# A row-wise log-sum-exp: the first piece's sum by way of PSUM, and two rows summed by halves instead of by a reduce

## The chip, the cores and the metric

The kernel runs on one core of a Trainium2 chip. The metric is device time in microseconds (us), from the start of the program to its end on that core; lower is better. Before the change it is 162.02 us, the median of three runs.

## What is computed

The input `x` is 32 x 512 x 1024 in float32, that is 16384 rows of 1024 elements. For each row:

```
max_x = np.max(x, axis=-1, keepdims=True)
out   = max_x.squeeze(-1) + np.log(np.sum(np.exp(x - max_x), axis=-1))
```

The kernel takes the exps without the maximum first and checks the sums. If every sum is between 1e-15 and 1e15, `log(sum(exp(x)))` is the answer; otherwise a second path, under an `If`, does the whole with the maximum. The data here never take that path.

## The kernel before

**Tiling.** Each of the 128 partitions has 128 rows (`NC`), numbered 0 to 127 in the order of loading; W = 112 divides them. Rows below 112 lie together in memory for each partition, and so do the last 16, so that the results go out in two stores. The on-chip buffer `ring` has room for 48 rows per partition. `LOADS` lists 18 loads with their size in rows and what is done with them. All are issued by SyncE (SP) on one DMA queue, the first six large (16 to 12.5 rows), the later ones ever smaller, down to about half a row. A load waits until the rows that it overwrites have been summed.

**What is done with a row.** ScalarE (ACT) takes the exp in place (L212), one instruction for each group of rows. Then the group is summed in one of these ways, each with a letter in `LOADS`:
- `R`: VectorE (DVE) reduces the rows whole, in one instruction (L223).
- `F`: GpSimd (POOL) adds the second half of each row to its first half (L217), "folds" it, and VectorE reduces the halves later (L159, in `reduce_folded`). The fold is put on a list; VectorE reduces what is on the list at the end of the next `R` or `T` group, or ahead of the next fold.
- `T`: VectorE takes the rows one by one: one instruction adds the two halves of a row and sums the result (L232), a 128x512 `SCALAR_TENSOR_TENSOR` with an accumulator. The accumulator is then read out to `sumexp` by an instruction of its own (`DVE_READ_ACCUMULATOR`).
- `Y` and `Z`: the last row, number 127, comes in two loads of 544 and 480 elements. ScalarE takes their exps into PSUM (`last_exp`) and sums them by its own accumulator (L190), which is read out by an `ACTIVATION_READ_ACCUMULATOR`: the first piece's sum to `sumexp[:, 127]`, the second's to `sumexp[:, 128]`.

**Order.** The code issues in the order of the loads, and each engine works through its own queue in that order; semaphores that count each engine's finished instructions tie them together. `Counted.wait` (L39 to L44) leaves a wait out if the engine has waited for the same count or a later one before. The ninth load, `(5.5, "F4 R2")`, holds rows 106 to 111, the last below W: four are folded, two reduced. From row 112 on, all groups but the last row are `T`: 4, 3, 3, 2, 1, 1 and 1 rows.

**The end.** When the groups up to row 118 are issued, ScalarE takes the Ln of rows 0 to 111 (L251), SyncE stores them (L259), and VectorE checks the sums of rows 0 to 118 (L134, L139). TensorE counts: each later row's sum is added up over the partitions in the PSUM tile `count` (`add_up`, L148), and so is the number of sums that were out of bounds (`bad`, L144 and L280). After the last row, ScalarE takes the Ln of rows 112 to 126 (L262) and of row 127 (L264, with the first piece's sum as bias), and SyncE stores the 16 columns (L268). VectorE checks rows 119 to 127 (L274), TensorE adds what is left, and VectorE compares the count with its bound (`fine`, L283). ScalarE and VectorE load that truth value, branch, and tell SyncE, which waits for the stores and ends the program.

Of the kernel before, what the change touches and what calls it, by code (L numbers as in the profile page):

```python
# [16 lines left out]

LOADS = [
# [3 lines left out]
]  # L22

# [24 lines left out]
def kernel(  # L48
# [5 lines left out]
    nc = tc.nc  # L54
# [4 lines left out]
    P = nc.NUM_PARTITIONS  # L59
    fp32 = mybir.dt.float32  # L60
# [8 lines left out]
    NC = n // P  # L69
    H = d // 2  # L70
    W = NC - B
    LAST = NC - 1
# [6 lines left out]
    def source(e0, size):  # L79
        assert e0 >= W * d or e0 + size <= W * d  # L80
        return x_rest[:, e0 - W * d : e0 - W * d + size] if e0 >= W * d else x_rows[:, e0 : e0 + size]
# [8 lines left out]
    def sbuf(name, cols, dtype=fp32, rows=P):  # L90
        return nc.alloc_sbuf_tensor(name, [rows, cols], dtype).ap()

    ring = sbuf("ring", RING * d)
    sumexp = sbuf("sumexp", NC + 1)
# [4 lines left out]
    ones = sbuf("ones", 1)  # L99
    fine = sbuf("fine", 1, i32, 1)  # L100
    last_exp = nc.alloc_psum_tensor("last_exp", [P, d], fp32).ap()
    count = nc.alloc_psum_tensor("count", [1, 1], fp32).ap()

    landed = [nc.alloc_semaphore(f"landed{i}") for i in range(len(loads))]
    act = Counted(nc, nc.scalar, "act")
    dve = Counted(nc, nc.vector, "dve")
# [15 lines left out]
    def load(i, here, done_before, size):  # L122
        for a, b, who, at in users:
            if a < here + size and b > here:
                sp.wait(who, at)
        users[:] = [u for u in users if not (u[0] < here + size and u[1] > here)]
        return nc.sync.dma_start(  # L127
            out=ring[:, here : here + size], in_=source(done_before, size)
        ).then_inc(landed[i], 16)

    def check_early():
        dve.wait(act, summed_by_act)
        dve.wait(dve, dve.n)
        dve.did(nc.vector.tensor_scalar(  # L134
            out=clamped[:, 0:LATE], in0=sumexp[:, 0:LATE],
            scalar1=LOW, scalar2=HIGH, op0=ALU.max, op1=ALU.min,
        ))
        dve.wait(dve, dve.n)
        dve.did(nc.vector.scalar_tensor_tensor(  # L139
            out=clamped[:, 0:LATE], in0=clamped[:, 0:LATE], scalar=0.0, in1=sumexp[:, 0:LATE],  # L140
            op0=ALU.bypass, op1=ALU.not_equal, accum_out=bad[:, 0:1],
        ))
        pe.wait(dve, dve.n)
        pe.did(nc.tensor.matmul(count, lhsT=bad[:, 0:1], rhs=far, start=True, stop=False))  # L144

    def add_up(c, who, **kw):
        pe.wait(*who)
        return pe.did(nc.tensor.matmul(count, lhsT=ones, rhs=sumexp[:, c : c + 1], **kw))  # L148
# [3 lines left out]
    def reduce_folded():  # L152

        nonlocal early_sum
        while folded:
            c0, s0, p0, n0 = folded.pop(0)
            halves = ring[:, p0 : p0 + s0 * d].rearrange("p (c d) -> p c d", d=d)[:, :, 0:H]
            dve.wait(pool, n0)
            at = dve.did(nc.vector.reduce_sum(  # L159
                out=sumexp[:, c0 : c0 + s0], in_=halves, axis=AX.X  # L160
            ))
            users.append((p0, p0 + s0 * d, dve, at))
            if c0 < W:
                early_sum = at

    c = 0
# [7 lines left out]
    for i, (size, ops) in enumerate(loads):  # L174
        if here + size > RING * d:
            assert here == p
            p = here = 0
        if any(q < here + size and q + t * d > here for _, t, q, _ in folded):
            reduce_folded()
        dma = load(i, here, done_before, size)  # L180
        first_load = first_load or dma.ins
        end = here + size
        done_before += size
        act.wait(landed[i], 16)
        for k, (how, s) in enumerate(ops):
            rows = ring[:, p : p + s * d].rearrange("p (c d) -> p c d", d=d)
            if how in "YZ":

                assert c == LAST and (how == "Z" or here == p)
                at = act.did(nc.scalar.activation(  # L190
                    out=last_exp[:, here - p : end - p], in_=ring[:, here:end], func=AF.Exp,
                    accum_out=sumexp[:, LAST : NC] if how == "Y" else sumexp[:, NC : NC + 1],
                ))
                here = end
                if how == "Y":
                    first_piece = at
                summed_by_act = at
            elif how == "A":
                assert here == p
                v = ring[:, p : p + d]  # L200
                at = act.did(nc.scalar.activation(
                    out=v, in_=v, func=AF.Exp, accum_out=sumexp[:, c : c + 1]
                ))
                here += d
                users.append((p, p + d, act, at))
                summed_by_act = at
                who = (act, at)
            else:

                upto = end if k + 1 == len(ops) and c + s < LAST else p + s * d  # L210
                v = ring[:, here:upto]
                at = act.did(nc.scalar.activation(out=v, in_=v, func=AF.Exp))  # L212
                here = upto
            if how == "F":
                reduce_folded()
                pool.wait(act, at)
                at = pool.did(nc.gpsimd.tensor_tensor(  # L217
                    out=rows[:, :, 0:H], in0=rows[:, :, 0:H], in1=rows[:, :, H:d], op=ALU.add
                ))
                folded.append((c, s, p, at))  # L220
            elif how == "R":
                dve.wait(act, at)
                who = (dve, dve.did(nc.vector.reduce_sum(  # L223
                    out=sumexp[:, c : c + s], in_=rows, axis=AX.X
                )))
                users.append((p, p + s * d, *who))
            elif how == "T":
                reduce_folded()
                dve.wait(act, at)
                for r in range(s):  # L230
                    lo = rows[:, r, 0:H]
                    who = (dve, dve.did(nc.vector.scalar_tensor_tensor(  # L232
                        out=lo, in0=lo, scalar=1.0, in1=rows[:, r, H:d],
                        op0=ALU.mult, op1=ALU.add, accum_out=sumexp[:, c + r : c + r + 1],
                    )))
                    users.append((p + r * d, p + (r + 1) * d, *who))
                    if c + r >= LATE:
                        add_up(c + r, who, start=False, stop=False)
            if how == "A" and c >= LATE:
                add_up(c, who, start=False, stop=False)  # L240
            if how in "RT":
                if c < W:
                    early_sum = dve.n
                reduce_folded()
            c += s
            p += s * d
            if c == LATE:

                act.wait(dve, early_sum)
                act.wait(act, early_act)  # L250
                ln_early = act.did(nc.scalar.activation(  # L251
                    out=res[:, 0:W], in_=sumexp[:, 0:W], func=AF.Ln
                ))
                check_early()
            if c <= W:
                early_act = summed_by_act
        assert here == end
# [7 lines left out]
        out=res[:, LAST:NC], in_=sumexp[:, NC : NC + 1], func=AF.Ln, bias=sumexp[:, LAST:NC]  # L265
# [3 lines left out]

    dve.wait(act, first_piece)
    dve.wait(dve, dve.n)
    dve.did(nc.vector.scalar_tensor_tensor(  # L274
        out=clamped[:, LATE:NC], in0=sumexp[:, LATE:NC], scalar=LOW,
        in1=sumexp[:, LATE:NC], op0=ALU.max, op1=ALU.not_equal, accum_out=bad[:, 1:2],
    ))
    add_up(LAST, (act, first_piece), start=False, stop=False)
    pe.wait(dve, dve.n)
    pe.did(nc.tensor.matmul(count, lhsT=bad[:, 1:2], rhs=far, start=False, stop=False))  # L280
    at = add_up(NC, (act, summed_by_act), start=False, stop=True)
    dve.wait(pe, at)
    at = dve.did(nc.vector.tensor_scalar(out=fine, in0=count, scalar1=HIGH, scalar2=None, op0=ALU.is_lt))  # L283
# [6 lines left out]
    with nc.If(all_fine < 1):  # L290
# [5 lines left out]
        for c0 in range(0, NC, RING):  # L296
# [6 lines left out]
            for c1, c2 in ((c0, edge), (edge, c0 + s)):  # L303
                if c1 == c2:
                    continue
                nc.scalar.dma_start(
                    out=ring[:, (c1 - c0) * d : (c2 - c0) * d],
                    in_=source(c1 * d, (c2 - c1) * d),
# [4 lines left out]
                out=neg, in_=v, op=ALU.max, axis=AX.X, negate=True  # L313
# [3 lines left out]
                out=v, in0=v, in1=neg[:, :, None].to_broadcast([P, s, d])  # L317
# [5 lines left out]
                out=sumexp[:, c0 : c0 + s], in_=v, axis=AX.X  # L323
# [71 lines left out]
```

## Time and profile before

| | us |
|---|---|
| median of three runs | 162.02 (161.79, 162.02, 163.18) |
| the profiled execution | 161.82 |
| its span, first to last instruction | 160.5 |
| VectorE busy in the span | 113.8 |
| ScalarE busy | 114.5 |
| GpSimd busy | 37.2 |
| mean DMA rate over the span | 419 GB/s |

An engine's busy time is the time in which it worked on an instruction. Where an instruction begins before the one ahead of it has left the pipeline, the two overlap in the list, so that a row's length is more than the distance to the next row's start. The timeline lists instructions in order of their start, with their length, their engine, the line of the code, and the output and input tiles; in brackets stands how long the engine was idle before and for whom it waited.

### The profile page before, as it was taken

The numbers are of one execution on the slowest core, as the hardware profiler recorded it, in microseconds if no ns is written. First come the engines' busy times: TensorE is split into PE (matmuls) and PEld (weight loads), VectorE is DVE, ScalarE is ACT, GpSimd is POOL, SyncE is SP. The second block draws the span as 40 slices with busy tenths as digits, with TensorE's granted clock in tenths as the row PEclk, the third lists the DMA queues.
The fourth block names the chain that finished last, engine by engine and source line by source line (L and its number), as shares of the span: only waits on it lengthen the run. The fifth ranks groups of instructions, "written<-read, shape, count | busy, mean of one in ns | idle before, by whom it ended". The sixth has DMA issues, their size and how long they took to land.

```text
span 160.5 us, 208 instructions
## 1 busy us (share of the span) xinstructions
PE 2.1 (1%) x24; PEld 1.0 (1%) x24; DVE 113.8 (71%) x53; ACT 114.5 (71%) x30; POOL 37.2 (23%) x10
## 2 busy tenths in 40 slices
PE   0000000000000000000000000000000000000022
PEld 0000000000000000000000000000000000000011
DVE  0000000009999499994999859959999999999995
ACT  3000059990799708995099949992999979989996
POOL 0000000000000000000000993690004969873000
DMA  8996996996996996996999999999999999999992
GB/s 278 506 523 278 506 523 261 523 523 261 523 523 261 523 506 278 523 490 294 482 441 441 441 425 408 408 408 498 423 423 404 406 426 421 449 406 427 417 407 80
DMA packets 2880, 67.18 MB, mean 419 GB/s; under 512 B 576, under 2 KB 704, under 8 KB 1344
## 3 DMA queue, kind: packets, MB, share of 16 engines
q1 hardware_dynamic: 2880, 67.18, 97.7%
HBM read 67.11 MB, written 0.07 MB: 419 GB/s over the span
## 4 chain that ended last, share of the span: by engine, by line
DMA 55%; DVE 22%; ACT 20%; SPq 0%; issue 0%; PE 0%; DVEq 0%
DMA ring<-in_x_dram 55%; ACT ring L212 20%; DVE sumexp L223 15%; DVE ring L232 4%; DVE sumexp L159 2%; SPq L127 0%; DVE clamped L139 0%; DVE clamped L134 0%; PE count L148 0%; PE count L280 0%; DVE clamped L274 0%; DVE fine L283 0%; DVEq L44 0%
## 5 line engine op out<-in xcount | busy, mean ns | idle before, releaser
L212 ACT ACTIVATE ring<-ring 128x16384 f32<-128x16384 f32 (+16 forms) x22 | 111.6, 5121 | 43.1 <-DMA ring<-in_x_dram 43.1
L223 DVE TENSOR_REDUCE sumexp<-ring 128x16 f32<-128x16384 f32 (+4 forms) x9 | 85.6, 9514 | 43.1 <-ACT ring L212 43.1
L217 POOL TENSOR_TENSOR ring<-ring 128x2048 f32<-128x2048 f32 (+2 forms) x6 | 37.0, 6171 | 108.5 <-ACT ring L212 108.5
L159 DVE TENSOR_REDUCE sumexp<-ring 128x4 f32<-128x2048 f32 (+2 forms) x6 | 18.4, 3078 | 0.1
L232 DVE SCALAR_TENSOR_TENSOR ring<-ring 128x512 f32<-128x512 f32 x15 | 9.5, 687 | 0.0
L115 ACT ACT_TABLE_LOAD x1 | 1.3, 1283 | 1.4 <-PEq L57 1.4
L144 PE MATMUL count<-far,bad 128*1 128x1 f32 x2 | 0.2, 164 | 153.3 <-DVE clamped L139 153.3
L148 PE MATMUL count<-sumexp,ones 128*1 128x1 f32 x20 | 1.8, 164 | 3.5 <-DVE ring L232 3.4
L232 DVE DVE_READ_ACCUMULATOR ring<-ring 128x1 f32 x15 | 1.2, 83 | 0.0
L190 ACT ACTIVATE last_exp<-ring 128x544 f32<-128x544 f32 (+1 forms) x2 | 1.2, 578 | 0.0
L116 DVE MEMSET ones<- 128x1 f32 x1 | 0.1, 59 | 1.5 <-PEq L57 1.5
L144 PEld LDWEIGHTS count<-far,bad 128*1 128x1 f32 x2 | 0.1, 82 | 153.3 <-DVE clamped L139 153.3
L148 PEld LDWEIGHTS count<-sumexp,ones 128*1 128x1 f32 x20 | 0.8, 81 | 4.4 <-DVE ring L232 4.3
L283 DVE TENSOR_SCALAR fine<-count 1x1 int32<-1x1 f32 x1 | 0.1, 145 | 0.5 <-PE count L148 0.5
L190 ACT ACTIVATION_READ_ACCUMULATOR last_exp<-ring 128x1 f32 x2 | 0.4, 186 | 0.0
L139 DVE SCALAR_TENSOR_TENSOR clamped<-clamped,sumexp 128x119 f32<-128x119 f32 x1 | 0.3, 283 | 0.0
L264 ACT ACTIVATE res<-sumexp 128x1 f32<-128x1 f32 x1 | 0.3, 294 | 0.0
L251 ACT ACTIVATE res<-sumexp 128x112 f32<-128x112 f32 x1 | 0.3, 280 | 0.0
L134 DVE TENSOR_SCALAR clamped<-sumexp 128x119 f32<-128x119 f32 x1 | 0.2, 223 | 0.0
L274 DVE SCALAR_TENSOR_TENSOR clamped<-sumexp 128x9 f32<-128x9 f32 x1 | 0.2, 169 | 0.1
L262 ACT ACTIVATE res<-sumexp 128x15 f32<-128x15 f32 x1 | 0.2, 198 | 0.0
L280 PE MATMUL count<-far,bad 128*1 128x1 f32 x2 | 0.2, 164 | 0.0
(8 smaller groups left out, 0.7 us busy)
## 6 DMA issues: line engine op xcount, KB each, us to landing
ring<-in_x_dram SPq DMA_DIRECT2D x1, 6912.0 KB, 23.9
ring<-in_x_dram SPq DMA_DIRECT2D x1, 6400.0 KB, 19.7
ring<-in_x_dram SPq DMA_DIRECT2D x1, 4608.0 KB, 15.9
ring<-in_x_dram SPq DMA_DIRECT2D x1, 3840.0 KB, 12.4
ring<-in_x_dram SPq DMA_DIRECT2D x1, 2816.0 KB, 18.7
ring<-in_x_dram SPq DMA_DIRECT2D x1, 2352.0 KB, 23.8
ring<-in_x_dram SPq DMA_DIRECT2D x1, 1664.0 KB, 21.1
ring<-in_x_dram SPq DMA_DIRECT2D x1, 1280.0 KB, 23.7
```

The costliest lines, as they stand in the source:

```text
L115: nc.scalar.preload_act_table_set("natural_log_exp_and_others")
L139: dve.did(nc.vector.scalar_tensor_tensor(out=clamped[:, 0:LATE], in0=clamped[:, 0:LATE], scalar=0.0, in1=sumexp[:, 0:LATE], op0=ALU.bypass ...
L144: pe.did(nc.tensor.matmul(count, lhsT=bad[:, 0:1], rhs=far, start=True, stop=False))
L148: return pe.did(nc.tensor.matmul(count, lhsT=ones, rhs=sumexp[:, c : c + 1], **kw))
L159: at = dve.did(nc.vector.reduce_sum(out=sumexp[:, c0 : c0 + s0], in_=halves, axis=AX.X))
L190: at = act.did(nc.scalar.activation(out=last_exp[:, here - p : end - p], in_=ring[:, here:end], func=AF.Exp, accum_out=sumexp[:, LAST : NC ...
L212: at = act.did(nc.scalar.activation(out=v, in_=v, func=AF.Exp))
L217: at = pool.did(nc.gpsimd.tensor_tensor(out=rows[:, :, 0:H], in0=rows[:, :, 0:H], in1=rows[:, :, H:d], op=ALU.add))
L223: who = (dve, dve.did(nc.vector.reduce_sum(out=sumexp[:, c : c + s], in_=rows, axis=AX.X)))
L232: who = (dve, dve.did(nc.vector.scalar_tensor_tensor(out=lo, in0=lo, scalar=1.0, in1=rows[:, r, H:d], op0=ALU.mult, op1=ALU.add, accum_out ...
L251: ln_early = act.did(nc.scalar.activation(out=res[:, 0:W], in_=sumexp[:, 0:W], func=AF.Ln))
L264: ln_last = act.did(nc.scalar.activation(out=res[:, LAST:NC], in_=sumexp[:, NC : NC + 1], func=AF.Ln, bias=sumexp[:, LAST:NC]))
```

## The change

The ninth load's two rows ahead of row 112 become a `T` group: two instructions that add halves and sum, instead of one reduce. The four folded rows of the same load are still reduced after them: for a `T` group ahead of row 112 the list of folds isn't emptied first. The sum of the last row's first piece (`Y`) is read out to a new PSUM tile, `first_sum`, instead of to `sumexp[:, 127]`. VectorE copies it from there to `sumexp[:, 127]`, behind the last `T` row on its queue, once ScalarE has it. VectorE's wait for ScalarE ahead of L274 goes, since the copy has waited, and TensorE, which adds that column up, waits for the copy instead of for ScalarE.

```diff
@@ -17,7 +17,7 @@
 
 LOADS = [
     (16, "R16"), (16, "R16"), (16, "R16"), (16, "F9 R7"), (13.5, "F6 R7"), (12.5, "R7 F6"),
-    (9, "R5 F4"), (7.5, "F4 R3"), (5.5, "F4 R2"), (4.59375, "T4"), (3.25, "T3"), (2.5, "T3"),
+    (9, "R5 F4"), (7.5, "F4 R3"), (5.5, "F4 T2"), (4.59375, "T4"), (3.25, "T3"), (2.5, "T3"),
     (1.78125, "T2"), (1.25, "T1"), (0.9375, "T1"), (0.6875, "T1"), (0.53125, "Y"), (0.46875, "Z"),
 ]
 
@@ -99,6 +99,7 @@
     ones = sbuf("ones", 1)
     fine = sbuf("fine", 1, i32, 1)
     last_exp = nc.alloc_psum_tensor("last_exp", [P, d], fp32).ap()
+    first_sum = nc.alloc_psum_tensor("first_sum", [P, 1], fp32).ap()
     count = nc.alloc_psum_tensor("count", [1, 1], fp32).ap()
 
     landed = [nc.alloc_semaphore(f"landed{i}") for i in range(len(loads))]
@@ -189,11 +190,12 @@
                 assert c == LAST and (how == "Z" or here == p)
                 at = act.did(nc.scalar.activation(
                     out=last_exp[:, here - p : end - p], in_=ring[:, here:end], func=AF.Exp,
-                    accum_out=sumexp[:, LAST : NC] if how == "Y" else sumexp[:, NC : NC + 1],
+                    accum_out=first_sum if how == "Y" else sumexp[:, NC : NC + 1],
                 ))
                 here = end
                 if how == "Y":
-                    first_piece = at
+                    dve.wait(act, at)
+                    first_piece = dve.did(nc.vector.tensor_copy(out=sumexp[:, LAST:NC], in_=first_sum))
                 summed_by_act = at
             elif how == "A":
                 assert here == p
@@ -225,7 +227,8 @@
                 )))
                 users.append((p, p + s * d, *who))
             elif how == "T":
-                reduce_folded()
+                if c >= W:
+                    reduce_folded()
                 dve.wait(act, at)
                 for r in range(s):
                     lo = rows[:, r, 0:H]
@@ -269,13 +272,12 @@
 
 
 
-    dve.wait(act, first_piece)
     dve.wait(dve, dve.n)
     dve.did(nc.vector.scalar_tensor_tensor(
         out=clamped[:, LATE:NC], in0=sumexp[:, LATE:NC], scalar=LOW,
         in1=sumexp[:, LATE:NC], op0=ALU.max, op1=ALU.not_equal, accum_out=bad[:, 1:2],
     ))
-    add_up(LAST, (act, first_piece), start=False, stop=False)
+    add_up(LAST, (dve, first_piece), start=False, stop=False)
     pe.wait(dve, dve.n)
     pe.did(nc.tensor.matmul(count, lhsT=bad[:, 1:2], rhs=far, start=False, stop=False))
     at = add_up(NC, (act, summed_by_act), start=False, stop=True)
```

## The prediction

> **What bounds the kernel now.** I read the chain of waits first, to learn which engine sets the end and from when. The chain in order of time (start, length, what), last half:
>
> ```profile
> 115.75 3.27 DVE sumexp L159
> ...
> 119.88 23.82 DMA ring<-in_x_dram
> 143.70 0.02 issue
> 143.72 7.00 ACT ring L212 x2
> 150.72 0.02 issue
> 150.75 1.94 DVE ring L232 x6
> ...
> 153.26 4.96 DVE ring L232 x16
> ...
> 158.32 0.19 DVE clamped L274 x2
> ...
> 158.98 0.14 DVE fine L283
> ```
>
> Up to 143.70 the loads set the pace. From there the exps (L212) run back to back, and the rows that VectorE (DVE) sums by halves (L232) follow close behind them, so the end has two chains that finish together. One is the check: the last row sum, L274, two pairs of matmuls, `fine` at 158.98. The other is the store, and it needs the timeline of the last stretch (start, length, engine, line):
>
> ```profile
> 157.51 0.69 DVE L232 SCALAR_TENSOR_TENSOR ring<-ring 128x512 f32<-128x512 f32 x1
> ...
> 157.93 0.19 ACT L190 ACTIVATION_READ_ACCUMULATOR last_exp<-ring 128x1 f32 x1
> 158.02 0.55 ACT L190 ACTIVATE last_exp<-ring 128x480 f32<-128x480 f32 x1
> 158.12 0.08 DVE L232 DVE_READ_ACCUMULATOR ring<-ring 128x1 f32 x1
> ...
> 158.60 0.20 ACT L262 ACTIVATE res<-sumexp 128x15 f32<-128x15 f32 x1
> 158.73 0.29 ACT L264 ACTIVATE res<-sumexp 128x1 f32<-128x1 f32 x1
> ...
> 159.05 0.34 SPq L268 DMA_DIRECT2D out_dram<-res  x1
> ```
>
> The list of DMA issues gives this last store 1.4 us to landing: 159.05 + 1.4 = 160.45, the span's 160.5. The check's chain has 160.5 - 159.12 = 1.4 us left after `fine` for the load of the truth value, the branch and SyncE's closing waits. Nothing shows more than a few hundredths of slack on either, so I take both as limiting. On the store's chain VectorE has room: its last row sum is out at 158.12 + 0.08 = 158.20 and ScalarE (ACT) asks for it at 158.60, 0.40 later.
>
> Then the place of the second edit, the timeline before the first L232:
>
> ```profile
> 141.40 4.54 POOL L217 TENSOR_TENSOR ring<-ring 128x2048 f32<-128x2048 f32 x1 [1.72 <-ACT ring L212]
> 141.44 2.28 DVE L159 TENSOR_REDUCE sumexp<-ring 128x4 f32<-128x2048 f32 x1
> 143.63 2.28 DVE L223 TENSOR_REDUCE sumexp<-ring 128x2 f32<-128x2048 f32 x1
> 143.72 6.99 ACT L212 ACTIVATE ring<-ring 128x4704 f32<-128x4704 f32 x2 [0.60 <-DMA ring<-in_x_dram]
> 145.97 2.29 DVE L159 TENSOR_REDUCE sumexp<-ring 128x4 f32<-128x2048 f32 x1
> 148.18 0.68 DVE L232 SCALAR_TENSOR_TENSOR ring<-ring 128x512 f32<-128x512 f32 x1
> 148.78 0.08 DVE L232 DVE_READ_ACCUMULATOR ring<-ring 128x1 f32 x1
> ```
>
> GpSimd (POOL) folds four rows of the 5.5-row load from 141.40 to 141.40 + 4.54 = 145.94. VectorE reduces the other two at 143.63 (the piece that changes), and at 145.97, 0.03 after POOL, reduces the folded four. The rows by halves begin at 148.18. POOL is done for good by then: in the whole trace no L232 lies beside an L217.
>
> **The two rows by halves.** Removed: one reduce, 143.63 to 145.91, 2.28 us. Added: two L232 with their accumulator reads; rows follow one another by 149.40 - 148.78 = 0.62, over several rows 0.612, so 1.22 us. No DMA is added, and all loads are issued by then, so no ring space is freed for anything. VectorE is 2.28 - 1.22 = 1.06 less busy, but that can't be a gain: the next instruction on its queue is the reduce of the folded rows, and that waits for POOL until 145.94 anyway. The cover of the saved 1.06 is POOL's fold; the most that can come forward is 0.03.
>
> The unknown is what POOL's fold and the two rows do to each other, since they now lie side by side. Lower bound: nothing. The nearest row is L223 beside L217: POOL's three folds of this size take 4.53 to 4.55 whatever VectorE reduces meanwhile, and the reduce of 2048 elements takes 2.28 both with POOL running (141.44) and without (145.97). Upper bound: the two exclude each other, and the rows' 1.22 us is added to POOL's 145.94. It does not matter which gives way: if the rows wait they run from 145.94 to 147.16, and if POOL waits its fold ends at 147.16. Below nothing there is only the 0.03.
>
> I take the upper bound, for a reason that lies in the rows. A reduce draws 2048 elements in 2.28 us, 1.11 ns each. L232 draws two halves, 1024 elements, in 0.612 us, 0.60 ns each. So L232 reads by a second path that the reduce leaves idle, and the undisturbed reduces say nothing of that path. POOL's fold draws 4096 elements in 4.54 us, 1.11 ns each, the rate of one path all the time. If the second path of VectorE is the one that POOL uses, there is little room in it for both.
>
> [...]
>
> With the upper bound the reduce of the folded rows starts at 147.16 + 0.03 = 147.19 instead of 145.97, 1.22 late. Who waits behind it: the Ln of the first 112 rows (L251) needs it, but ScalarE only comes to it at 150.62, and the reduce ended at 148.26, so 2.36 us of cover hide the delay. All L232 rows are queued behind it. They start at 149.40 and run without a pause until the end, since the exps are then ahead. Two small waits for ScalarE swallow part: the fifth row could start at 150.62 (rows start with the accumulator read of the one before) and did at 150.75, 0.13; the last could at 157.46 and did at 157.51, 0.05. So 1.22 - 0.18 = 1.04 arrives at the last row sum: 158.20 becomes 159.24.
>
> **The first piece's sum by way of PSUM.** The accumulator read of L190 now writes PSUM; the row lasts 0.19 either way as far as the trace can say, and the next exp starts 0.09 after its start, so I cost it at nothing. Added: a copy of 128x1 on VectorE, behind the last row and ahead of L274. The trace has no such copy. Bounds: 0.06 (L116's 128x1 memset, 59 ns) and 0.145 (L283, which reads PSUM); I take 0.145, since this one reads PSUM too. The last row's accumulator read starts at 158.12 + 1.04 = 159.16, the copy with it, and ends at 159.31; a wait on VectorE's own result costs 0.04 (152.67 to L134 at 152.71), so L274 starts at 159.35. Before, L274 paid for two waits, 158.20 to 158.32; now the wait for ScalarE sits on the copy. Queued behind the copy's wait are only L274 and `fine`; the wait itself is over at 158.12, long before.
>
> **The sum.** Check: L274 at 159.35 for 158.32, +1.03; the matmuls and `fine` follow, as L280 started at 158.55 on L274's result and the next pair at 158.75 right after it. Store: L262 now waits for the copy too, 159.35 for 158.60, +0.75. The check ends last; with some hundredths of slack that it may have had against the store, +1.0. The profiled execution took 161.82 (span 160.5), so 162.8; the median of the runs, 162.02, is 0.2 above that execution, so 163.0.
>
> **The rivals.**
> - Hidden: rows and fold pass each other freely, price zero. For it: the reduces beside POOL. Against: the rate of reading. The folded rows are then reduced at 145.97 as now. The copy waits for the first piece (158.12), runs 158.16 to 158.31, L274 at 158.35, +0.03, and the store does not feel it (158.35 against 158.60): 162.05. This is the case that ends not slower.
> - Partly shared: POOL leaves the path free for part of the time and is late by about half, 0.6. Then 0.6 - 0.18 + 0.03 = +0.45, 162.5.
> - Worse than taking turns: each hand-over loses time. It decides beyond 1% when the fold is late by over 1.62 + 0.18 = 1.8 us, and once it is late by more than 2.36 the Ln at L251 stops ScalarE and all exps with it. 163.8 or more. Nothing in the trace speaks for it, as each of the two rows would have to cost about 0.9 instead of 0.61.
> - The change gives time back: the accumulator's way to PSUM ends sooner, and the 0.03 comes forward. At most 0.1: 161.9. A gain over 1% has no place to come from, since ScalarE runs without a gap from the landing at 143.70 to 159.02.
>
> **How the numbers follow.** Taking turns 0.62, hidden 0.20, partly shared 0.09, worse 0.07, a little time back 0.02. The forecast is the likeliest case, 163.0. The range goes down to the hidden case, less its scatter, and up by 0.4 for a copy or hand-over that costs more and for the scatter of the runs (161.79 to 163.18): 161.9 to 163.4. Faster or slower by over 1% (1.62 us, about what a measurement of this kernel can tell from no change): slower 0.07 from the worse case and 0.03 from the tail of the forecast's own, 0.10; faster 0.02; within 1% 0.88.
>
> **What the profile after would show.** Right: the first L232 near 143.6 lasting some 3 us or starting at 145.9, or POOL's last fold lasting near 5.8; L159's last reduce at 147.2; the first of the four rows at 149.4; L274 at 159.3; L262 later than 158.6 and waiting for VectorE. Wrong: POOL's last fold at 4.54, both L232 done by 145, and L159 at 145.97 again; then the hidden case holds. If L159 starts at 147.2 and the span is still 160.5, my reading that the rows run without a pause behind it is what failed.

## The result, and the profile after

The changed kernel takes 162.48 us (median of 22 runs, 162.33 to 164.06); the kernel before took 161.91 beside it (22 runs, 161.74 to 163.41). The ratio is 1.0044, 95% interval 1.0024 to 1.0063: 0.57 us slower by the medians. The forecast was 163.0. (A ratio given here and below is not the quotient of the two medians beside it; the two differ by up to 0.3%.)

First the place of the rows by halves, the timeline of the changed kernel (start, length, engine, line):

```profile
141.51 4.53 POOL L219 TENSOR_TENSOR ring<-ring 128x2048 f32<-128x2048 f32 x1 [1.74 <-ACT ring L214]
141.55 2.28 DVE L160 TENSOR_REDUCE sumexp<-ring 128x4 f32<-128x2048 f32 x1
143.74 2.86 DVE L235 SCALAR_TENSOR_TENSOR ring<-ring 128x512 f32<-128x512 f32 x1
143.83 6.99 ACT L214 ACTIVATE ring<-ring 128x4704 f32<-128x4704 f32 x2 [0.59 <-DMA ring<-in_x_dram]
...
146.53 0.68 DVE L235 SCALAR_TENSOR_TENSOR ring<-ring 128x512 f32<-128x512 f32 x1
147.14 0.08 DVE L235 DVE_READ_ACCUMULATOR ring<-ring 128x1 f32 x1
147.14 2.27 DVE L160 TENSOR_REDUCE sumexp<-ring 128x4 f32<-128x2048 f32 x1
149.34 0.68 DVE L235 SCALAR_TENSOR_TENSOR ring<-ring 128x512 f32<-128x512 f32 x1
```

The loads of this execution landed 0.11 later than those of the one before (POOL starts at 141.51, not 141.40), so 0.11 comes off each start when the two are compared. The first row by halves lasts 2.86 us where others last 0.68: it began at 143.74, in the middle of POOL's fold, and finished 0.56 after the fold's end at 146.04. POOL's 4.53 is unchanged. The second row follows at once, and the reduce of the folded rows starts at 147.14 instead of 145.97, less 0.11: 1.06 late. This wait does not appear as idle time in the list, since the instruction has started; it appears as one instruction of the group that is far longer than its kind.

Then the end of the same timeline:

```profile
158.49 0.68 DVE L235 SCALAR_TENSOR_TENSOR ring<-ring 128x512 f32<-128x512 f32 x1
158.57 0.19 ACT L191 ACTIVATION_READ_ACCUMULATOR last_exp<-ring 128x1 f32 x1
...
159.10 0.15 DVE L198 COPY sumexp<-first_sum 128x1 f32<-128x1 f32 x1
...
159.28 0.21 ACT L265 ACTIVATE res<-sumexp 128x15 f32<-128x15 f32 x1 [0.52 <-DVE sumexp L198]
159.28 0.17 DVE L276 SCALAR_TENSOR_TENSOR clamped<-sumexp 128x9 f32<-128x9 f32 x1
...
159.51 0.09 PEld L282 LDWEIGHTS count<-far,bad 128*1 128x1 f32 x2
...
159.54 0.11 PEld L149 LDWEIGHTS count<-sumexp,ones 128*1 128x1 f32 x2
...
159.71 0.34 SPq L271 DMA_DIRECT2D out_dram<-res  x1
159.79 0.15 DVE L285 TENSOR_SCALAR fine<-count 1x1 int32<-1x1 f32 x1 [0.33 <-PE count L149]
```

ScalarE now stands idle for 0.52 ahead of the Ln of rows 112 to 126 (L265), which it did not before, and waits for the copy behind VectorE's late last row. The store is issued at 159.71 instead of 159.05, less 0.11: 0.55 late, which is nearly the whole of the 0.57. SyncE's own waits say which of the two chains closes the program. Before, it waited at the end for VectorE's report alone:

```profile
SPq L339 <- DVEq L336: 0.9, 1, 0.9
```

In the changed kernel:

```profile
SPq L341 <- DVEq L338: 0.7, 1, 0.7
...
SPq L343 <- SPq L343: 0.3, 1, 0.3
```

L341 waits for the end of the check, L343 after it for the store. The 0.3 at L343 had no counterpart before: in this execution the store is last, by 0.2 to 0.3, where the two were level.

### The profile page after: what moved, and what is told of

It is laid out like the page before. It is cut to its first block, busy times and chain, and to the rows that moved or that the text cites. A ratio compares the mean times of both kernels' runs of the same rounds, so it can differ in the third digit from the quotient of the medians.

```text
span 161.2 us, 211 instructions
## 1 busy us (share of the span) xinstructions
PE 2.0 (1%) x24; PEld 1.0 (1%) x24; DVE 114.8 (71%) x57; ACT 114.5 (71%) x30; POOL 37.2 (23%) x10
## 4 chain that ended last, share of the span: by engine, by line
DMA 47%; DVE 30%; ACT 20%; PE 0%; issue 0%
DMA ring<-in_x_dram 47%; ACT ring L214 20%; DVE sumexp L225 18%; DVE ring L235 8%; DVE sumexp L160 5%; PE count L149 0%; DVE clamped L140 0%; DVE clamped L135 0%; PE count L282 0%; DVE fine L285 0%
## 5 line engine op out<-in xcount | busy, mean ns | idle before, releaser
L225 DVE TENSOR_REDUCE sumexp<-ring 128x16 f32<-128x16384 f32 (+3 forms) x8 | 83.4, 10419 | 43.2 <-ACT ring L214 43.2
L235 DVE SCALAR_TENSOR_TENSOR ring<-ring 128x512 f32<-128x512 f32 x17 | 12.8, 811 | 0.0
L265 ACT ACTIVATE res<-sumexp 128x15 f32<-128x15 f32 x1 | 0.2, 215 | 0.5 <-DVE sumexp L198 0.5
L254 ACT ACTIVATE res<-sumexp 128x112 f32<-128x112 f32 x1 | 0.3, 280 | 0.0
L276 DVE SCALAR_TENSOR_TENSOR clamped<-sumexp 128x9 f32<-128x9 f32 x1 | 0.2, 169 | 0.0
L282 PE MATMUL count<-far,bad 128*1 128x1 f32 x2 | 0.2, 164 | 0.0
```

The lines of the kernel that those rows point to most:

```text
L225: who = (dve, dve.did(nc.vector.reduce_sum(out=sumexp[:, c : c + s], in_=rows, axis=AX.X)))
L235: who = (dve, dve.did(nc.vector.scalar_tensor_tensor(out=lo, in0=lo, scalar=1.0, in1=rows[:, r, H:d], op0=ALU.mult, op1=ALU.add, accum_out ...
L254: ln_early = act.did(nc.scalar.activation(out=res[:, 0:W], in_=sumexp[:, 0:W], func=AF.Ln))
```

## The experiments

The theory was that rows by halves and POOL's fold take turns, and that all of the cost lies there. The first rival was that the copy and its wait at the end cost the time; the second, that this kind of instruction waits for POOL whatever it reads. Each ratio below is to the kernel before, beside which it ran.

### The first piece's sum alone

```diff
-    (9, "R5 F4"), (7.5, "F4 R3"), (5.5, "F4 T2"), ...
+    (9, "R5 F4"), (7.5, "F4 R3"), (5.5, "F4 R2"), ...
```

> Only the first piece's way by PSUM with its copy; the two rows stay one reduce. Taking turns (two rows by halves and POOL's fold exclude each other, all of the cost lies there): the last reduce of folded rows starts 0.03 us after POOL's fold ends, and the time is that of before, 161.9, at most 0.05 below it because the second piece's exp starts 0.05 instead of 0.09 after the accumulator read. Rival, the copy and its wait at the end are the cost: about 162.4 here.

Measured: 161.85, before 161.81, ratio 0.9984 (0.996 to 1.0008). The copy is not the cost. In the timeline of this kernel's end its 0.15 us starts with the last row's accumulator read and is over at 158.21, before ScalarE asks at 158.50:

```profile
157.87 0.11 ACT L191 ACTIVATION_READ_ACCUMULATOR last_exp<-ring 128x1 f32 x1
157.92 0.55 ACT L191 ACTIVATE last_exp<-ring 128x480 f32<-128x480 f32 x1
158.06 0.08 DVE L235 DVE_READ_ACCUMULATOR ring<-ring 128x1 f32 x1
158.06 0.15 DVE L198 COPY sumexp<-first_sum 128x1 f32<-128x1 f32 x1
...
158.25 0.17 DVE L276 SCALAR_TENSOR_TENSOR clamped<-sumexp 128x9 f32<-128x9 f32 x1
...
158.50 0.20 ACT L265 ACTIVATE res<-sumexp 128x15 f32<-128x15 f32 x1
```

The accumulator read into PSUM takes 0.11 instead of 0.19, and the next exp starts 0.05 after it instead of 0.09. These few hundredths are below what the comparison can tell.

### The two rows alone

```diff
-    ... (5.5, "F4 R2"), ...
+    ... (5.5, "F4 T2"), ...
             elif how == "T":
-                reduce_folded()
+                if c >= W:
+                    reduce_folded()
```

> Only the two rows by halves; the first piece's sum goes straight to SBUF, no copy. Taking turns: the first of the two rows lasts about 2.9 us, the last reduce of folded rows starts 1.1 us after POOL's end, and the time is that of the changed kernel less the copy's 0.15 on the store's path: 162.35. Rival, the copy is the cost: 161.9.

Measured: 163.16, before 161.81, ratio 1.007 (1.0045 to 1.0095). The rows are where they were expected (the first lasts 2.86, the reduce of the folded rows starts 1.1 after POOL's end), and the store was issued at 159.55, earlier than in the changed kernel. Yet the program ended 0.7 later than that. The list of DMA queues and issues shows what is different:

```profile
q14 instruction: 1, 0.01, 0.0%
...
out_dram<-res SPq DMA_DIRECT2D x1, 8.0 KB, 2.2
```

The last store took 2.2 us to land, not 1.4, and one packet of 8 KB came in on the queue of kind "instruction". In the trace it runs from 160.40 to 160.82. Of the store's 144 packets 135 are done by 160.60, and nine run only from 160.82 to 160.88, when that packet is through; I take these nine to be on the DMA engine that carried it (144 is nine for each of 16). Their wait is only 0.28 of the 0.8. The rest comes behind them: the landing is reported in 16 parts, of which 15 are in by 160.97 and the last one comes at 161.75. The packet is taken up again below.

### The same rows, second operand in PSUM

```diff
     dve.did(nc.vector.memset(far, 100 * HIGH))
+    dve.did(nc.vector.memset(last_exp, 1.0))
...
-                        out=lo, in0=lo, scalar=1.0, in1=rows[:, r, H:d],
+                        out=lo, in0=lo, scalar=1.0, in1=last_exp[:, 0:H] if c < W else rows[:, r, H:d],
```

> The changed kernel, but in the two rows ahead of row 112 the second operand is a PSUM tile filled with ones at the start, so that the sums of these two rows leave out their second halves. Same instruction, same length, same place beside POOL's fold, one SBUF input instead of two. Taking turns over a path that only the second SBUF input needs: both rows last 0.7 and are done by 145, the last reduce of folded rows starts 0.03 after POOL's end, 161.9. Rival, this kind of instruction (two inputs, an accumulator) waits for POOL whatever it reads: first row 2.9 us, 162.5.

The timeline of this kernel beside the fold:

```profile
141.33 4.54 POOL L220 TENSOR_TENSOR ring<-ring 128x2048 f32<-128x2048 f32 x1 [1.74 <-ACT ring L215]
141.37 2.28 DVE L161 TENSOR_REDUCE sumexp<-ring 128x4 f32<-128x2048 f32 x1
143.56 0.68 DVE L236 SCALAR_TENSOR_TENSOR ring<-ring,last_exp 128x512 f32<-128x512 f32 x1
...
144.16 0.68 DVE L236 SCALAR_TENSOR_TENSOR ring<-ring,last_exp 128x512 f32<-128x512 f32 x1
144.77 0.08 DVE L236 DVE_READ_ACCUMULATOR ring<-ring,last_exp 128x1 f32 x1
145.90 2.29 DVE L161 TENSOR_REDUCE sumexp<-ring 128x4 f32<-128x2048 f32 x1 [1.05 <-POOL ring L220]
```

These rows settle what waits. The instruction, its size and its place beside the fold are the same; only its second input comes from PSUM instead of SBUF, the on-chip memory that holds `ring`, and it runs in 0.68 while POOL works, not in 2.86. So it is the second input from SBUF that waits. The reduce of the folded rows then waits 1.05 for POOL, as the hidden case of the prediction had it.

The time, 162.33 (161.89 to 163.35), before 161.81, ratio 1.0024 (0.9994 to 1.0054), did not come down to 161.9 as expected. In the profiled execution the last exp waited 0.66 for the last load, and an 8 KB packet of kind "instruction" ran at 156.86, among the last loads.

### The rows behind the fold

```diff
-                if c >= W:
-                    reduce_folded()
+                reduce_folded()
```

> The changed kernel, but the folded rows are reduced ahead of the two rows by halves, so that these come when POOL is done. Taking turns: no long row; the reduce starts 0.03 after POOL's end, both rows follow at 0.61, and the rows of the next load start some 0.1 to 0.2 later than in the changed kernel: 162.5 to 162.65. Rival, lying beside POOL costs more than the two rows' own length: faster than the changed kernel, 162.2 or less.

Measured: 162.50, before 161.81, ratio 1.0026 (1.0002 to 1.005). The timeline of VectorE shows no long row:

```profile
145.95 2.29 DVE L160 TENSOR_REDUCE sumexp<-ring 128x4 f32<-128x2048 f32 x1 [2.25 <-POOL ring L219]
148.15 0.68 DVE L234 SCALAR_TENSOR_TENSOR ring<-ring 128x512 f32<-128x512 f32 x1
...
149.37 0.69 DVE L234 SCALAR_TENSOR_TENSOR ring<-ring 128x512 f32<-128x512 f32 x1
```

The next load's rows start at 149.37, 1.19 later than in the kernel before (148.18); in the changed kernel they start 1.05 later (149.34, less 0.11). So beside POOL or behind it, the two rows cost about the same: nearly their own length, 1.22, while the reduce that they replace ran during the fold and delayed nothing. Nothing further is lost by the meeting itself.

### An additional GpSimd addition among the rows

```diff
+                    if c + r == 119:
+                        pool.wait(pool, extra_set)
+                        pool.wait(*who)
+                        pool.did(nc.gpsimd.tensor_tensor(
+                            out=extra[:, 0:512], in0=extra[:, 0:512], in1=extra[:, 512:1024], op=ALU.add
+                        ))
...
+    nc.sync.wait_ge(pool.sem, pool.n)
     nc.sync.wait_ge(done, 2)
```

> The kernel before, with an additional GpSimd addition of 128x512 on a tile that nothing else uses, started once row 119 is summed, among the rows by halves. Taking turns: alone it would last about 1.3 us (from the folds' 4.54 at 2048 and 6.73 at 3072 elements); it starts while a row runs, and the next row ends that much later; the tail moves by 1.2 to 1.3, and with 0.4 of room for the store the time is 162.7 to 162.9. Rival, they pass each other freely: rows at 0.61, 161.9.

Measured: 162.73, before 161.86, ratio 1.0088 (1.0055 to 1.012). The timeline of POOL alone shows the additional instruction:

```profile
153.93 1.58 POOL L242 TENSOR_TENSOR extra<-extra 128x512 f32<-128x512 f32 x1 [8.06 <-DVE ring L234]
```

The timeline of VectorE alone shows the rows around it:

```profile
153.69 0.69 DVE L234 SCALAR_TENSOR_TENSOR ring<-ring 128x512 f32<-128x512 f32 x1
154.31 0.08 DVE L234 DVE_READ_ACCUMULATOR ring<-ring 128x1 f32 x1
154.31 1.76 DVE L234 SCALAR_TENSOR_TENSOR ring<-ring 128x512 f32<-128x512 f32 x1
...
155.99 0.68 DVE L234 SCALAR_TENSOR_TENSOR ring<-ring 128x512 f32<-128x512 f32 x1
```

Here the row came first, and POOL's addition takes 1.58. By the estimate of 1.3 from the folds' lengths (4.54 at 2048 elements, 6.73 at 3072; no run shows this addition alone) about 0.3 of that is a wait for the row that is running. The next row, beside the addition, takes 1.76 instead of 0.68. POOL works on another tile and in another stretch, so the turn isn't a matter of `ring`.

### One row by halves, one reduced

```diff
-    ... (5.5, "F4 T2"), ...
+    ... (5.5, "F4 R1 T1"), ...
-                reduce_folded()
+                if c >= W or k + 1 == len(ops):
+                    reduce_folded()
```

> The changed kernel with one of the two rows reduced (128x1024, ahead) and only the other by halves. Taking turns: the reduce is done by 144.9, the row waits for POOL and ends 0.5 after it, the last reduce of folded rows starts 0.5 late, 0.18 of which the two small waits swallow, and the rest fits into the store's 0.4 of room less the copy: 161.9 to 162.05. Rival, a price for each such row: half of the change's 0.57, 162.2.

Measured: 161.97, before 161.86, ratio 1.001 (0.9999 to 1.0021). The row and the reduce of the folded rows in the timeline:

```profile
144.74 1.74 DVE L235 SCALAR_TENSOR_TENSOR ring<-ring 128x512 f32<-128x512 f32 x1
...
146.41 2.27 DVE L160 TENSOR_REDUCE sumexp<-ring 128x4 f32<-128x2048 f32 x1
```

The reduce starts 0.45 late, and the store is issued at 159.00, no later than before (159.05). The price is not proportional: one row costs 0.1, if anything, and two cost 0.57, because the two small waits (0.18) and the store's 0.4 of room, less the copy's 0.15, swallow the first row's delay.

### Three rows by halves, one load earlier

```diff
-    (9, "R5 F4"), (7.5, "F4 R3"), ...
+    (9, "R5 F4"), (7.5, "F4 T3"), ...
```

> The kernel before, with the three reduced rows of the load before (7.5 rows) taken by halves, beside POOL's fold of 135.1 to 139.7; the 5.5-row load as before, no PSUM sum. Taking turns: the first of the three rows starts at 138.2 and ends about 0.5 after POOL's end, the three are done by 141.4, when the reduce was done too, so nothing moves: 161.9. Rival, rows by halves ahead of row 112 cost about 0.28 each wherever they are: 162.7.

The timeline of this kernel beside the fold of the load before:

```profile
135.12 4.52 POOL L217 TENSOR_TENSOR ring<-ring 128x2048 f32<-128x2048 f32 x1 [0.22 <-ACT ring L212]
...
138.16 2.03 DVE L233 SCALAR_TENSOR_TENSOR ring<-ring 128x512 f32<-128x512 f32 x1 [0.40 <-ACT ring L212]
...
141.35 2.27 DVE L159 TENSOR_REDUCE sumexp<-ring 128x4 f32<-128x2048 f32 x1
```

The turn is there again (2.03 for the first row, which ends 0.55 after POOL), and as expected it moves nothing: the reduce starts at 141.35, the reduce of the last folded rows at 145.97, and the store is issued at 159.03, 159.05 before. But the time is 162.35, before 161.86, ratio 1.0024 (1.0013 to 1.0036). This expectation missed, and so would the rival's price have. The last store took 1.9 to land, and an 8 KB packet of kind "instruction" ran from 159.41 to 159.96, across the store's first packets at 159.87. Again 15 of the store's 16 reports are in by 160.45, and one comes at 160.95.

### The packet on the instruction queue

In three runs the time was off beside a packet that no line of the kernel issues. It lay inside the program in all kernels whose trace has 66 or more VectorE instructions, waits and branches counted (the changed kernel 66, at 157.11; the two rows alone 66, at 160.40; the rows behind the fold 66, at 157.14; PSUM operand 67, at 156.86; three rows earlier 68, at 159.41), and after the last instruction in all with 65 or fewer (the kernel before 63, at 160.91, where the span ends at 160.5). The expectations below call it a code fetch; that is a guess from the name of the queue's kind, and no trace shows what the packet carries. So I changed this count and as little else as I could. In three kernels the memsets of `ones` and `far` at the start went to GpSimd, two VectorE instructions fewer; in the kernel before, three memsets were added:

```diff
-    dve.did(nc.vector.memset(ones, 1.0))
-    dve.did(nc.vector.memset(far, 100 * HIGH))
+    pool.did(nc.gpsimd.memset(ones, 1.0))
+    consts_set = pool.did(nc.gpsimd.memset(far, 100 * HIGH))
...
+        pe.wait(pool, consts_set)
         pe.wait(dve, dve.n)
```

```diff
     dve.did(nc.vector.memset(far, 100 * HIGH))
+    for k in range(3):
+        dve.did(nc.vector.memset(spare[:, k : k + 1], 1.0))
```

The two rows alone, with two fewer:

> The two rows by halves without the PSUM sum, as in the run that took 163.16, but the two memsets at the start (ones, far) are GpSimd's instead of VectorE's: two VectorE instructions fewer, nothing else. Theory, a code fetch: that run's last 0.8 us is an 8 KB packet on the instruction queue that met the last store (it landed 2.2 us after its issue instead of 1.4), and it comes inside the program once VectorE has some 66 instructions in it, where 65 and 63 had none. With two fewer the packet is outside the span, the last store lands after 1.4, and the time is 162.35 to 162.4. Rival, the two rows delay the last store in another way: 163.1 to 163.2 as before.

Measured: 162.50, where it was 163.16; before 161.87, ratio 1.0026 (1.0004 to 1.0048). No such packet is inside the span, and the last store lands after 1.4. That it is 0.1 above what was expected comes from the check, which ends last here: SyncE waits 1.1 for VectorE's report and not at all for the store.

The kernel before, with three more:

> The kernel before with three further memsets of one column at the start, on VectorE, which nothing uses: 66 VectorE instructions instead of 63. Theory, a code fetch: an 8 KB packet on the instruction queue appears inside the span; where it falls isn't known, so 161.9 (if it meets no store and no late load) to 162.7 (if it meets the last store, which then lands more than 1.4 after its issue). Rival, the packet belongs to the rows by halves and not to the count: none inside the span, 161.8 to 161.9.

Measured: 162.49, before 161.87; ratio 1.0025 (1.0 to 1.005). Three memsets of one column, nearly 160 us ahead of the end, cost 0.6 by the medians; the interval reaches down to no change, but the list of queues and issues shows the packet and the late store:

```profile
q14 instruction: 1, 0.01, 0.0%
...
out_dram<-res SPq DMA_DIRECT2D x1, 8.0 KB, 1.8
```

The packet runs from 159.61 to 160.11. The store's packets are not late here: the last one ends 1.05 after the issue, as in the kernel before. What is late is again one report of the 16, at 160.99, when the other 15 are in by 160.55.

The PSUM operand, with two fewer:

> The rows whose second operand is in PSUM (the sums of two rows leave out their second halves), again with the two memsets at the start on GpSimd. Theory, a code fetch: the 162.33 of that run was the last load, landed 0.7 late beside the fetched packet; with 65 VectorE instructions no packet falls into the span, the last exp isn't held up, and the time is that of the kernel before, 161.8 to 161.95. Rival, the rows themselves cost it: 162.3.

Measured: 161.83, before 161.87; ratio 0.9983 (0.996 to 1.0006). With the packet out of the program, a row by halves beside the fold costs nothing if its second input is in PSUM. This completes the third experiment. (The trace kept of this kernel is of an execution of 162.40, in which the loads landed about 0.6 late; the two rows last 0.68 in it too.)

The changed kernel, with two fewer:

> The changed kernel with the two memsets at the start on GpSimd. Theory, a code fetch: the packet that fell at 157 in the changed kernel, beside the last loads, moves out of the span; there it held up nothing that was read (the last loads landed at 157.5 as before), so the time stays at 162.4 to 162.5. If the packet cost something there after all: below 162.3.

Measured: 162.51, before 161.87, ratio 1.0038 (1.0011 to 1.0065): the same as the changed kernel. In the changed kernel the packet fell at 157.1 and held up no load that was waited for. This run and the one before it both have no packet inside the program and differ in the second operand of the two rows (and the memset that fills it): 162.51 against 161.83. So what the change costs is the turn-taking, not the packet.

The long row is as it was:

```profile
143.61 2.85 DVE L236 SCALAR_TENSOR_TENSOR ring<-ring 128x512 f32<-128x512 f32 x1
```

The end differs from the changed kernel's all the same. SyncE waits for VectorE's report and not for the store:

```profile
SPq L342 <- DVEq L339: 1.0, 1, 1.0
```

VectorE reports at 160.94, 0.65 later than in the kernel before (160.29), and the store lands at 161.00, 0.54 later. So which of the two chains ends last goes with the packet's place, while the time hardly does: they stay within 0.3 of each other.

None of these kernels is faster than the kernel before: the PSUM sum alone is level with it.

## Why the prediction was right, point by point

- **The two rows and the fold exclude each other.** Right. The second path of VectorE's reading, argued from 0.60 against 1.11 ns for an element, was my reading of the rates, and no trace shows such a path. What the rows show: beside the fold a reduce is left alone (2.28), a row with two SBUF inputs waits (2.86), and the same row with its second input in PSUM does not (0.68); beside the additional addition a row takes 1.76. The time alone would not have shown it: 162.48 is also what the case "partly shared" gives, 162.5. The rows rule that out, since the first one lasts until POOL is done, and POOL's 4.53 is unchanged.
- **1.22 late at the reduce of the folded rows.** Measured 1.06. By an estimate from the rows' spacing the first row got under way about 0.12 before POOL's recorded end: undisturbed rows follow one another by 0.61, the second row started at 146.53, and 146.53 - 0.61 = 145.92, against 146.04. The other kernels with such a row give 0.12 to 0.13 in the same way. The 0.03 between POOL's end and the reduce is gone as well.
- **0.18 swallowed by two small waits.** Right: 1.06 became 0.87 at the last row's accumulator read (159.10 less 0.11, for 158.12).
- **The Ln of the first 112 rows isn't held up.** Right: L254 ran at 150.72 with no idle time ahead of it.
- **The copy: 0.145, hidden.** Right: 0.15, and no cost when it is the only change. That the accumulator read takes as long into PSUM was wrong (0.11, not 0.19), without an effect on the time.
- **The sum.** By the store's chain, which stands beside the check's in the prediction, it would have been 162.02 + 0.75 = 162.8; with the row's real 1.06 it is 162.6. Another 0.11 of the excess is the start: 162.02 is the median of three runs, 161.91 that of 22. The range, 161.9 to 163.4, holds the 162.48, but it is wide enough to hold no change at all; what bears the mechanism out is the rows, not the number.
- **"The check ends last", +1.0.** Too large, and this is the step that failed. The check had slack that I did not see, in these lines of the kernel before:

```profile
158.51 0.19 ACT L190 ACTIVATION_READ_ACCUMULATOR last_exp<-ring 128x1 f32 x1
158.55 0.09 PEld L280 LDWEIGHTS count<-far,bad 128*1 128x1 f32 x2 [0.15 <-DVE clamped L274]
...
158.75 0.09 PEld L148 LDWEIGHTS count<-sumexp,ones 128*1 128x1 f32 x2
```

The last pair of matmuls (L148) started 0.20 after L280, and I read it as following L280; but it also waits for the second piece's sum, read out at 158.51 + 0.19 = 158.70. After, that sum is long there, and the pair follows L282 by 0.03. So `fine` was late by 159.79 - 158.98 - 0.11 = 0.70 while L276 was late by 0.85. Behind `fine`, VectorE went from the start of its load of the truth value to its report to SyncE in 0.79 us instead of 1.13, as in every trace here that has the instruction packet inside the program (0.78 to 0.80, against 1.09 to 1.21 in the others); why the two go together is not shown. So the check's report was only 0.37 late (160.77, less 0.11, for 160.29), and the store, priced at +0.75, was 0.55 late and ended last. Where the packet is outside the program (the changed kernel with two fewer), the check did end last, but by 0.65 instead of 1.0.

## What to carry to other kernels

Before a VectorE instruction is replaced by a shorter one, look at what GpSimd does at that moment: in these kernels an instruction that reads two SBUF operands waited for GpSimd's addition (2.86 us instead of 0.68), one that reads a single one (a reduce, 2.28 us beside the fold, 2.29 behind it), or its second one from PSUM (0.68), did not. A saving ahead of a wait that ends later anyway is worth nothing, while a delay there is worth everything beyond the slack. Where two chains end together, price both to the end, and find for each instruction of the last microsecond every wait that it has, not only the latest one.

## What the hardware showed that I had not expected

In these kernels one packet of 8 KB on the instruction queue, once late in the program, went with 0.5 to 0.7 us more by the medians where it ran shortly before or beside the last store's packets: 163.16 against 162.50 with two memsets moved to another engine, 162.49 against 161.87 with three added, 162.35 against 161.86 with three rows by halves earlier. In all three such traces one of the store's 16 reports of landing comes 0.4 to 0.8 us behind the other 15, as it would if one of the 16 DMA engines had carried the packet and was late with its share; the trace does not name the engines. The store's own packets wait 0.28 us at the most, and in one of the three not at all, so that what holds the report up behind them stays open. In these 13 kernels the packet fell inside the program exactly where VectorE had 66 instructions or more. When within the program it comes (156.9 to 160.4 here), and by which rule, stays open. A difference of half a microsecond between two versions of this kernel that differ in VectorE's instruction count can be this alone (162.49 against 161.87), so the queue list and the last store's time to landing are worth a look before any other cause is named.
